# Half of the first layer's modulation products as dot products on VectorE, woven with the other half on TensorE

## The chip, the cores and the metric

The kernel runs on one core of one Trainium2 chip. The metric is the device time of one execution in microseconds (us): 2820.16 us as the median of 3 runs of the kernel before, which lie between 2816.92 and 2826.93 us. Everything is computed in 32-bit floats, or in pairs of high and low parts that stand for them.

## The reference, cut to what matters

The network has two layers of a first kind (mixers of attention, retention and gated linear attention) and then two layers of a second kind (attention and a feed-forward part, with a context stream beside the main one). Each layer of the first kind scales and shifts its input, and gates its output, by three vectors that depend on a condition c alone:

```python
c_act = jax.nn.silu(c)                      # 1 x 1024
# in layer l:
mod = c_act @ w_mod[l] + b_mod[l]           # 1024 by 3072 matrix
shift, scale, gate = jnp.split(mod, 3)
h = rms_norm(x, pre_gain) * (1.0 + scale) + shift
... y = mixers(h @ w_in) @ w_out
x = x + gate * rms_norm(y, post_gain)
```

The second kind does the same with six vectors a layer out of `ada_w`, for a condition and for a context condition. So a layer of the first kind needs a vector times a 12 MB matrix, and the vector is the same all through. None of it depends on x, so it can be computed long before its layer begins.

## The kernel before, in words

Activations stand with the 1024 features in 8 groups of 128 partitions and the 512 tokens along the row. Each weight block of 128 outputs is loaded as 512 KB on SP's queue (`weights`, L413 to 425), split by ScalarE into a high part (`wh`) and by GpSimd or VectorE into a low part (`wl`), and multiplied three times for each group of features (`dense`, L389 is the line of every matmul).

The first layer's `start` computes its own shift and scale. All later modulation vectors are made in the background: `mods` (L732) is a generator, and each call of `tick` from the loop that weaves the foreground work (`weave`) adds a rate to a counter and takes as many steps of the generator as the counter holds. A step is one load of the matrix on SP's queue (L750) into a tile `mr` of 128 partitions by 4 by 256 floats, 512 KB, from a ring of three. Two of them hold 256 columns of the matrix for all 1024 rows. `mod_sum` (L708) multiplies them on TensorE: the condition vector, in 32 columns of which one or two are used, is the weight, the matrix streams past, and four strips of 32 partitions of one PSUM tile hold partial sums. The second piece is multiplied first. `mod_take` (L719) copies the sums to SBUF on ScalarE (`ms`), `mod_cols` (L724) adds the strips and turns them into columns with small matmuls by `mod_sel`, and VectorE adds the bias (L741). Both PSUM tiles are of the tag `b`, which has two buffers for the whole kernel; the pairwise products of the gated linear attention use the same two.

During the first layer, `run` gives the background 24 such blocks: 4 for the gate of layer 0 (group 2 of `w_mod[0]`), 12 for all of layer 1 (groups 1, 0, 2 of `w_mod[1]`) and 8 for the first two groups of `ada_w[0]`, one after the other, at 0.76 steps per tick. In the foreground stand the gated linear attention (`gla`), woven with the projections and the retention (`layer1`), and after it the windowed attention, woven with half of the output projection. The gated linear attention goes through pairs of tiles: GpSimd multiplies (L1116, `pg`), ScalarE and VectorE split into `qb` (L1100, L400), TensorE multiplies into a `b` tile, VectorE copies it under a mask into the accumulator (L1135, `oy`). The results of the background are needed when the boundary to layer 1 (gate of layer 0, shift and scale of layer 1) and the norm of the context stream begin; the ring belongs to a memory area (`mp`) that is closed before that.

The order in each engine's queue is not the order of the program text alone: a planner goes through the instructions by priority (the order of the text, with shifts by hand), with costs of its own for each, and gives out the buffers of a ring as they come free in its own account of time. The engines then run their queues in that fixed order.

Of the kernel before, what the change touches and what calls it, by code (L numbers as in the profile page):

```python
# [11 lines left out]
F32 = mybir.dt.float32  # L12
# [4 lines left out]
AF = mybir.ActivationFunctionType  # L17
ALU = mybir.AluOpType
# [4 lines left out]
D = 1024  # L23
KD = D // 128
# [24 lines left out]
def _block1_cols():  # L49
    r = np.arange  # L50
    o = O1
    fm = [o["gq"] + r(128), o["gk"] + r(128)]
    fm += [heads(o["rq"], range(4), X1A), heads(o["rq"], range(4), X2A)]
    fm += [heads(o["rk"], range(4), X1A), heads(o["rk"], range(4), X2A)]
    fm += [np.r_[heads(o["ak"], range(2), X1A), heads(o["ak"], range(2), X2A)]]
    for g in range(2):
        fm += [heads(o["aq"], range(4 * g, 4 * g + 4), X1A), heads(o["aq"], range(4 * g, 4 * g + 4), X2A)]
    fm += [o["gg"] + i * 128 + r(128) for i in range(2)]
    fm += [o["rg"] + i * 128 + r(128) for i in range(2)]
    fm += [o["ag"] + i * 128 + r(128) for i in range(4)]  # L60
    tm = [np.r_[o["gv"] + r(256), o["ga"] + r(16)], np.r_[o["rv"] + r(256), o["av"] + r(128)]]
    return fm, tm
# [31 lines left out]
def _modw(w, n=256):  # L94

    return w.reshape(KD, 128, -1, n).transpose(2, 1, 0, 3)


def _modw_start(w):
# [9 lines left out]
def _xt(x):  # L109
    return x.reshape(x.shape[-2], KD, 128).transpose(2, 1, 0)  # L110
# [89 lines left out]
class Net:  # L200
# [531 lines left out]
    def mods(self, m, wsrc, groups):  # L732
        nc = self.nc
        outs, b, vecs = m

        def finish(t, g, q):
            o = self.mod_cols(t)
            w = slice(g * KD + 2 * q, g * KD + 2 * q + 2)
            for i, (_, n) in enumerate(vecs):
                if g < n:  # L740
                    nc.vector.tensor_add(outs[i][:, w], o[:, :, i], b[:, w])  # L741

        last = None
        for g in groups:
            for q in range(4):
                pieces = []
                for p in range(2):
                    raw = self.tl(self.mp, [128, 4, 256], F32, "mr", 3)
                    yield
                    nc.sync.dma_start(raw, wsrc[4 * g + q, :, 4 * p:4 * p + 4, :])  # L750
                    pieces.append(raw)
                t = self.mod_take(self.mod_sum(pieces, vecs, (1, 0)), self.mp, 2)
                if last is not None:
                    finish(*last)
                last = t, g, q
        yield
        finish(*last)

    def gain1(self, gain, scale, name):

        t = self.common.tile([128, KD], F32, tag=name, name=name)
        self.nc.vector.scalar_tensor_tensor(t, scale, 1.0, gain, op0=ALU.add, op1=ALU.mult)
        return t
# [1006 lines left out]
    def run(self):  # L1770
        nc, I = self.nc, self.I
# [4 lines left out]
        m1 = self.mod1  # L1776
        ada = [self.mods_new(I["ada_b"][l], 6, [("c_2", 6), ("c_ctx_2", (6, 2)[l])], f"ada{l}") for l in range(2)]
        m, mc = (self.mods2(0, ada[0][0][i], "xy"[i]) for i in range(2))
        with self.phase("c1") as self.c1:
            self.cp = self.vp = self.c1  # L1780
            mp = self.phase("mp")
            self.mp = mp.__enter__()
            self.background(self.chain(self.mods(m1[0], I["w_mod"][0], (2,)), self.mods(m1[1], I["w_mod"][1], (1, 0, 2)),
                                       self.mods(ada[0], I["ada_w"][0], (1, 0))), 0.76)
            mix = self.run_through(self.layer1(0, h, ready))
            self.stage(low=3)
            self.setup2()
            self.drain()
            mp.__exit__(None, None, None)
            with self.phase("ctx") as ph:  # L1790
                done = {}
                with self.phase("xc") as px:
                    xc = px.tile([128, KD, CL], F32, name="xc0")
                    nc.sync.dma_start(xc, I["ctx"])
                    y, sq = self.weave((self.out_proj(I["w_out"][0], mix[0], S, *mix[1:]), 8, 0),
                                       (self.keep(done, self.prenorm_steps(xc, CL, *mc(0), pool=ph)), 9, 0))
                scc, win, lat = self.even_project(done["result"], CL, 0, False, ph)
                h = self.weave((self.boundary(y, sq, I["x"], self.post_mod1(0), self.pre_mod1(1), x1), 18, 0), (win(), 4.5, -200))
                self.close_y()
                layer = self.layer1(1, h, {})  # L1800
                self.weave((self.first(layer, 3), 3, -200), (lat(), 11.0, 0))
            self.stage(low=3, mods=300)
            with self.phase("mp") as self.mp:
                self.background(self.mods(ada[0], I["ada_w"][0], (2,)), 0.5)
                mix = self.run_through(layer)
                self.drain()
        self.stage(low=3)
        with self.phase("c2") as self.c2:
# [3 lines left out]
            mp = self.phase("mp")  # L1812
# [16 lines left out]
            with self.phase("evp") as ph:  # L1829
                sc, win, lat = self.even_project(h, S, CL, True, ph)  # L1830
                self.weave((win(), 4.8, 0), (self.postnorm_steps(xc, yc, sqc, CL, mc(1)), 12.0, 0))
                o = self.oy(S)
# [25 lines left out]
            m, mc = (self.mods2(1, ada[1][0][i], "xy"[i]) for i in range(2))  # L1858
            with self.phase("ctx") as cx:
                with self.phase("ffn") as ph:  # L1860
# [3 lines left out]
                    f = self.ffn(0, h, S, hid)  # L1864
# [4 lines left out]
                _, val, diff, keys, _ = self.odd_project(done["result"], CL, 0, False, cx)  # L1869
# [3 lines left out]
        with self.phase("odd") as ph:  # L1873
            o = self.oy(S)
# [42 lines left out]
def _layout(a):  # L1917
    f1, (ta, tb) = _block1_cols()
    sq = np.arange(D).reshape(KD, 128)
    fo, to = _odd_cols()  # L1920
    uq = [np.concatenate([96 * h + np.arange(64) for h in (2 * i, 2 * i + 1)]) for i in range(4)]
    uq += [np.concatenate([96 * h + 64 + p for h in range(8)]) for p in (P1, P2)]
    ukv = np.concatenate([128 * h + np.arange(64) for h in range(8)] + [128 * h + 64 + np.arange(64) for h in range(8)])
    qn = a["od_qk_norm_2"][0]
    r = {
        "x": _xt(a["x"]), "c": a["c"].reshape(KD, 128).T, "positions": a["positions"].reshape(1, S),
        "w_mod_start": _modw_start(a["w_mod"][0]),
        "w_mod": np.stack([_modw(w) for w in a["w_mod"]]),
        "b_mod": _vec(a["b_mod"], 3 * KD).transpose(1, 0, 2),
        "pre_gain": _vec(a["pre_norm_gain"]), "post_gain": _vec(a["post_norm_gain"]),  # L1930
        "w_in": np.stack([_fm(w, f1) for w in a["w_in"]]),
        "w_tok_a": np.stack([_units(w, ta) for w in a["w_in"]]),
        "w_tok_b": np.stack([_units(w, tb) for w in a["w_in"]]),
        "attn_sinks": a["attn_sinks"].reshape(1, 16),
        "gla_gate_w": a["gla_gate_w"], "gla_gate_b": a["gla_gate_b"],
        "gla_gain": np.tile(a["gla_norm_gain"], (1, 2)).T,
        "w_out": np.stack([_fm(w, sq) for w in a["w_out"]]),
        "c_2": a["c_2"].reshape(KD, 128).T, "c_ctx_2": a["c_ctx_2"].reshape(KD, 128).T,
        "ctx": _xt(a["ctx_2"]),
        "ada_w": np.stack([_modw(w) for w in a["ada_w_2"]]),  # L1940
        "ada_b": _vec(a["ada_b_2"], 6 * KD).transpose(1, 0, 2),
        "norm_g": a["norm_g_2"].reshape(2, 4, KD, 128).transpose(3, 0, 1, 2),
        "ffn_w_in": np.stack([_fm(w, np.arange(2 * FH).reshape(-1, 128)) for w in a["ffn_w_in_2"]]),
        "ffn_w_out": np.stack([_fm(w, sq) for w in a["ffn_w_out_2"]]),
        "ev_w_in": _fm(a["ev_w_in_2"][0], _even_cols()),
        "ev_sink": a["ev_sink_2"].reshape(1, 8),
        "mla_gain": np.concatenate([a["ev_q_norm_2"][0].reshape(2, 128), a["ev_kv_norm_2"]]).T,
        "ev_w_uq": _fm(a["ev_w_uq_2"][0], uq).transpose(1, 0, 2, 3),
        "ev_w_ukv": a["ev_w_ukv_2"][0][:, ukv],
        "ev_w_out": _fm(a["ev_w_out_2"][0], sq),  # L1950
        "od_w_in": _fm(a["od_w_in_2"][0], fo),
        "od_w_tok0": _units(a["od_w_in_2"][0], to[0]), "od_w_tok1": _units(a["od_w_in_2"][0], to[1]),
        "qk_gain": np.stack([np.tile(qn[0][X1B], 4), np.tile(qn[0][X2B], 4), np.tile(qn[1][X1B], 4),
                             np.tile(qn[1][X2B], 4), np.r_[np.tile(qn[1][X1B], 2), np.tile(qn[1][X2B], 2)]], 1),
        "od_lambda": a["od_lambda_2"].reshape(1, 256),
        "subln": a["od_subln_2"].T,
        "od_w_out": _fm(a["od_w_out_2"][0], sq),
    }
    r.update(_consts())
    return {k: np.ascontiguousarray(v) for k, v in r.items()}  # L1960
# [22 lines left out]
```

## Time and profile before

| what | value |
|---|---|
| median of 3 runs | 2820.16 us |
| the profiled execution | 2819.89 us |
| its span, first to last instruction | 2818.1 us |
| mean granted TensorE clock | 0.918 of full speed |
| loads of `w_mod` in the background | 32 of 512 KB, issued from 101.2 to 311.3 us |
| loads of `ada_w` in the background of the first layer | 16 of 512 KB, issued from 311.7 to 411.4 us |

Engines are called PE (TensorE), PEld (its weight loads), DVE (VectorE), ACT (ScalarE), POOL (GpSimd) and SP (the queue that issues the DMAs) in the profile. A group of instructions is named by the line of the kernel, the engine, the operation and what is written from what (`b<-mr,mc` is a PSUM tile `b` from a matrix piece and the condition vector). L389, L398 and L400 are lines of helpers that many places use; the names of the tiles tell these apart. A wait is put down to the engine whose signal came last.

### The profile page before, as it was taken

The page shows a single profiled execution, that of the slowest core. Times are in us where ns is not written, and L with a number is a line of the kernel's source. Part 1 is how long each engine was busy: PE and PEld are TensorE (multiplying, and loading weights), DVE is VectorE, ACT ScalarE, POOL GpSimd, SP SyncE. Part 2 cuts the span into 40 slices and gives each one's busy share as a digit, 9 for nine tenths or more (in the row PEclk, how much of TensorE's full clock was granted, in tenths as well). Part 3 has the DMA queues.
Part 4 walks back from the last instruction along what each step waited for, and adds up shares of the span by engine and source line. Part 5 has one row for each costly group of instructions (what it writes and reads, how often), then busy time and mean ns, then how long its engine had stood idle before and what let it go on. Part 6 is the DMA issues. An engine that isn't in the chain of part 4 may idle for free. (4 is left out here: it accounts for less than half of the span.)

```text
span 2818.1 us, 35394 instructions
## 1 busy us (share of the span) xinstructions
PE 2455.0 (87%) x13052; PEld 1994.9 (71%) x13052; DVE 1258.7 (45%) x2065; ACT 1188.2 (42%) x2227; POOL 1079.4 (38%) x754
## 2 busy tenths in 40 slices
PE   6988896778888886769999899999888989799997
PEld 4765666666666665648998777777776777688886
DVE  3655357235646644445442631212645767421212
ACT  3534365333547534445554522222434646332222
POOL 2435235344533551213455732322542222443334
PEclk9988998888979987879999999999988989899998
DMA  7364644344344652335553545454444253333332
GB/s 244 121 205 156 207 165 154 107 140 162 104 124 139 213 182 100 116 112 143 174 159 135 186 135 172 149 169 133 148 140 158 90 153 113 113 100 97 94 97 75
DMA packets 170816, 400.56 MB, mean 142 GB/s; under 512 B 19378, under 2 KB 60820, under 8 KB 167316
## 3 DMA queue, kind: packets, MB, share of 16 engines
q1 hardware_dynamic: 170644, 398.31, 43.7%
q8 instruction: 103, 1.69, 0.2%
q14 instruction: 69, 0.57, 0.1%
HBM read 339.85 MB, written 58.39 MB: 141 GB/s over the span
## 5 line engine op out<-in xcount | busy, mean ns | idle before, releaser
L398 POOL TENSOR_TENSOR wl<-wr,wh 128x1024 fp32r<-128x1024 f32 (+3 forms) x245 | 538.2, 2198 | 899.5 <-ACT wh L422 451.5
L422 ACT CAST wh<-wr 128x1024 fp32r<-128x1024 f32 (+3 forms) x367 | 353.8, 964 | 706.5 <-PE d L389 279.5
L389 PE MATMUL d<-hh,wh 128*128 128x512 f32 x960 | 398.4, 415 | 19.7 <-ACT hh L556 7.8
L389 PE MATMUL d<-hl,wh 128*128 128x512 f32 x960 | 394.0, 410 | 1.9 <-DVE hl L557 0.9
L389 PE MATMUL d<-hh,wl 128*128 128x512 f32 x960 | 263.5, 403 | 0.0
L400 DVE SCALAR_TENSOR_TENSOR wl<-wr,wh 128x1024 fp32r<-128x1024 f32 (+3 forms) x122 | 152.1, 1246 | 227.8 <-PE d L389 91.9
L389 PEld LDWEIGHTS d<-hh,wh 128*128 128x128 f32 x960 | 190.6, 199 | 62.2 <-ACT hh L556 8.4
L389 PEld LDWEIGHTS d<-hl,wh 128*128 128x128 f32 x960 | 189.7, 198 | 42.5 <-issue 2.5
L389 PEld LDWEIGHTS d<-hh,wl 128*128 128x128 f32 x960 | 185.0, 195 | 39.6 <-issue 1.6
L400 DVE SCALAR_TENSOR_TENSOR pg<-b,pg 128x512 fp32r<-128x512 f32 (+1 forms) x208 | 137.2, 665 | 68.7 <-ACT pg L404 67.2
L389 PE MATMUL b<-hh,wh 128*128 128x512 f32 x416 | 164.2, 395 | 0.0
L389 PE MATMUL b<-hl,wh 128*128 128x512 f32 x416 | 163.2, 392 | 0.0
L934 POOL TENSOR_TENSOR oy<-pg,pg 64x256 f32<-64x256 f32 (+1 forms) x72 | 57.7, 802 | 262.3 <-DVE pg L932 91.3
L404 ACT CAST pg<-b 128x512 fp32r<-128x512 f32 (+1 forms) x208 | 117.1, 570 | 80.2 <-PE b L909 68.2
L882 DVE TENSOR_REDUCE sm<-s 128x1 f32<-128x768 f32 (+3 forms) x144 | 120.7, 846 | 26.6 <-PE s L389 25.9
L389 PE MATMUL d<-hc,wh 128*128 128x256 f32 x656 | 105.4, 311 | 23.7 <-DVE rp L400 11.8
L950 DVE SCALAR_TENSOR_TENSOR rp<-rp,d 128x512 f32<-128x512 f32 (+1 forms) x77 | 46.7, 607 | 165.5 <-ACT rp L949 165.4
L1745 DVE SCALAR_TENSOR_TENSOR rp<-rp,b 128x512 f32<-128x512 f32 (+1 forms) x64 | 38.1, 595 | 175.3 <-PE b L389 174.8
L389 PE MATMUL d<-hid,wh 128*128 128x512 f32 (+1 forms) x528 | 114.7, 361 | 1.5 <-POOL hid L398 1.5
L389 PEld LDWEIGHTS d<-hc,wh 128*128 128x128 f32 x656 | 94.9, 211 | 28.3 <-ACT wh L422 12.2
L389 PE MATMUL b<-hid,wh 128*128 128x512 f32 (+1 forms) x528 | 110.8, 361 | 0.0
L389 PE MATMUL b<-hh,wl 128*128 128x512 f32 x416 | 103.8, 389 | 0.0
(416 smaller groups left out, 5143.2 us busy)
## 6 DMA issues: line engine op xcount, KB each, us to landing
wr<-in_ffn_w_in SPq DMA_DIRECT2D x132, 512.0 KB
mr<-in_ada_w SPq DMA_DIRECT2D x96, 512.0 KB
wr<-in_ffn_w_out SPq DMA_DIRECT2D x48, 512.0 KB
x<-x SPq DMA_DIRECT2D x20, 1024.0 KB
wr<-in_w_in SPq DMA_DIRECT2D x38, 512.0 KB
mr<-in_w_mod SPq DMA_DIRECT2D x32, 512.0 KB
wr<-in_ev_w_in SPq DMA_DIRECT2D x20, 512.0 KB
wr<-in_ffn_w_out SPq DMA_DIRECT2D x24, 384.0 KB
```

What stands on the lines that cost most here:

```text
L389: self.nc.tensor.matmul(out, lhsT, rhs, start=start, stop=stop)
L398: self.nc.gpsimd.tensor_sub(out, src, hi)
L400: self.nc.vector.scalar_tensor_tensor(out, src, scale, hi, op0=ALU.mult, op1=ALU.subtract)
L404: self.nc.scalar.copy(hi, src)
L422: nc.scalar.copy(hi[:, :n], raw[:, :n])
L882: nc.vector.reduce_max(c, s, axis=AX.X, negate=True)
L934: nc.gpsimd.tensor_tensor(d, sel(t), sel(rs), op=ALU.mult)
L950: nc.vector.scalar_tensor_tensor(t, t, 1.0, ps, op0=ALU.add, op1=ALU.mult)
L1745: nc.vector.scalar_tensor_tensor(g, g, 0.5, pu, op0=ALU.mult, op1=ALU.mult)
```

## The change

In the first layer's background the 12 blocks of layer 1 leave `mods`. A new generator, `mods_rows`, computes them as dot products. The matrix is laid out in memory by output (`w_mod_rows`: 24 slabs of 128 outputs by 1024 inputs), so an output is a partition and its inputs lie along the row. The condition vector is loaded once into all 128 partitions; ScalarE's Tanh and a VectorE operation make its activation. Each half slab (128 by 512 floats, 256 KB) is loaded into `mr`, and one VectorE operation multiplies it by the vector and writes the sum over the row into a column of the result, or of `part` for the second half; two small additions per group of eight columns add the bias and the second half. That is 48 loads and 48 such operations.

The other 12 blocks stay with `mods`, but in the first layer with pieces of two row groups (256 KB) instead of four, `self.mk = 2`, so a block takes four loads. Both generators are woven one step each, share one ring of four 256 KB buffers, and run at 1.55 steps per tick. After the first layer `mk` is 4, with 512 KB pieces in a ring of three as before; there, too, the pieces are now multiplied in the order in which they are loaded.

```diff
-                for p in range(2):
-                    raw = self.tl(self.mp, [128, 4, 256], F32, "mr", 3)
+                n = self.mk
+                for p in range(KD // n):
+                    raw = self.tl(self.mp, [128, n, 256], F32, "mr", (4, 3)[n // 4])
                     yield
-                    nc.sync.dma_start(raw, wsrc[4 * g + q, :, 4 * p:4 * p + 4, :])
+                    nc.sync.dma_start(raw, wsrc[4 * g + q, :, n * p:n * p + n, :])
                     pieces.append(raw)
-                t = self.mod_take(self.mod_sum(pieces, vecs, (1, 0)), self.mp, 2)
+                t = self.mod_take(self.mod_sum(pieces, vecs, range(KD // n)), self.mp, n // 2)
...
+    def mods_rows(self, m, wsrc, groups, src):
+
+        nc = self.nc
+        (out,), b, _ = m
+        row, t = self.tl(self.mp, [128, D], F32, "row", 1), self.tl(self.sb, [128, D], F32, "wr", 3)
+        nc.sync.dma_start(row, src.to_broadcast([128, D]))
+        nc.scalar.activation(t, row, AF.Tanh, scale=0.5)
+        nc.vector.scalar_tensor_tensor(row, t, 1.0, row, op0=ALU.add, op1=ALU.mult)
+        for g in groups:
+            w = slice(g * KD, g * KD + KD)
+            part = self.sm([128, KD])
+            for f in range(KD):
+                for p in range(2):
+                    raw = self.tl(self.mp, [128, D // 2], F32, "mr", 4)
+                    yield
+                    d = slice(D // 2 * p, D // 2 * (p + 1))
+                    nc.sync.dma_start(raw, wsrc[g * KD + f, :, d])
+                    o = part[:, f:f + 1] if p else out[:, g * KD + f:g * KD + f + 1]
+                    nc.vector.scalar_tensor_tensor(raw, raw, 0.5, row[:, d], op0=ALU.mult, op1=ALU.mult, accum_out=o)
+            nc.vector.tensor_add(out[:, w], out[:, w], b[:, w])
+            nc.vector.tensor_add(out[:, w], out[:, w], part)
...
-            self.mp = mp.__enter__()
-            self.background(self.chain(self.mods(m1[0], I["w_mod"][0], (2,)), self.mods(m1[1], I["w_mod"][1], (1, 0, 2)),
-                                       self.mods(ada[0], I["ada_w"][0], (1, 0))), 0.76)
+            self.mp, self.mk = mp.__enter__(), 2
+            by_rows = self.mods_rows(m1[1], I["w_mod_rows"], (1, 0, 2), I["c_row"])
+            by_cols = self.chain(self.mods(m1[0], I["w_mod"], (2,)), self.mods(ada[0], I["ada_w"][0], (1, 0)))
+            self.background(self.woven((by_rows, 48, 0), (by_cols, 51, 0)), 1.55)
...
             mp.__exit__(None, None, None)
+            self.mk = 4
```

## Rows read from the trace of the kernel before

**Rows 1.** The page, part 1: busy us, share, instructions.

```profile
PE 2455.0 (87%) x13052; PEld 1994.9 (71%) x13052; DVE 1258.7 (45%) x2065; ACT 1188.2 (42%) x2227; POOL 1079.4 (38%) x754
```

**Rows 2.** The chain of waits that ended last, by line, shares of the span.

```profile
by line: PE b L389 0.6%; PE d L389 0.5%; DVE bp L576 0.2%; DVE x L577 0.1%; PE s L498 0.0%; PE s L389 0.0%; POOL sm L483 0.0%; DVE oy L625 0.0%; ACT rp L503 0.0%; issue 0.0%; DVE sm L481 0.0%
```

**Rows 3.** Stretches 95:312 and 312:455, summed: busy us of each engine.

```profile
sum 360.00, PE 312.30 PEld 234.54 DVE 192.02 ACT 166.45 POOL 155.06; mean PE 156.15 PEld 117.27 DVE 96.01 ACT 83.22 POOL 77.53
```

**Rows 4.** The same view in 5 us steps, with PEclk, DMA share, GB/s.

```profile
140.00:145.00 5.00, 5.00 (x29) 4.75 (x28) 3.72 (x5) 3.53 (x8) 2.45 (x3) 1.00 0.79 264
160.00:165.00 5.00, 0.79 (x1) 0.29 (x1) 0.74 (x3) 2.01 (x5) 1.74 (x1) 0.55 0.91 329
440.00:445.00 5.00, 5.00 (x24) 4.14 (x23) 4.42 (x8) 2.92 (x6) 4.08 (x4) 1.00 0.30 105
```

**Rows 5.** TensorE's waits, 95 to 455 us: total us, times, longest.

```profile
PE b L389 <- DMA mr<-in_w_mod: 7.3, 3, 3.7
PE b L389 <- DVE oy L1135: 6.9, 5, 2.2
PE d L389 <- ACT wh L422: 5.9, 1, 5.9
PE b L498 <- DVE rp L495: 4.0, 2, 2.3
PE b L389 <- DVE rp L518: 3.3, 1, 3.3
PE b L389 <- DVE pg L1190: 3.2, 1, 3.2
...
PE d L389 <- DVE pg L400: 2.0, 3, 1.3
...
PE d L389 <- DVE rp L950: 1.7, 1, 1.7
```

**Rows 6.** TensorE's groups, 95 to 455 us: busy, mean ns | idle.

```profile
L389 PE MATMUL b<-mr,mc 128*32 128x256 f32 x384 | 35.7, 430 | 12.8 <-DMA mr<-in_w_mod 7.3 <-DVE pg L1190 3.2 <-DVE oy L1135 2.1
L389 PE MATMUL b<-mod_sel,ms 128*128 128x2 f32 x96 | 16.4, 276 | 0.3 <-DVE oy L1135 0.2
```

**Rows 7.** ScalarE's groups, the same view and stretch.

```profile
L721 ACT COPY ms<-b 128x256 f32<-128x256 f32 x24 | 8.9, 370 | 18.9 <-PE b L389 18.4
...
L887 ACT ACTIVATION_READ_ACCUMULATOR wp<-s,sm 128x1 f32 x32 | 6.6, 207 | 0.0
```

**Rows 8.** VectorE's groups, the same view and stretch.

```profile
L400 DVE SCALAR_TENSOR_TENSOR rp<-rp,rp 128x512 f32<-128x512 f32 x9 | 9.6, 1061 | 9.1 <-ACT rp L404 5.7 <-ACT rp L406 2.7
...
L400 DVE SCALAR_TENSOR_TENSOR pg<-b,pg 128x512 fp32r<-128x512 f32 x14 | 9.4, 681 | 2.5 <-ACT pg L404 2.5
...
L1313 DVE SCALAR_TENSOR_TENSOR oy<-oy,rp 128x512 f32<-128x512 f32 x8 | 5.4, 690 | 4.2 <-POOL oy L934 2.4 <-DMA rp<-gate 1.8
...
L400 DVE SCALAR_TENSOR_TENSOR wl<-wr,wh 128x512 fp32r<-128x512 f32 x5 | 3.7, 737 | 4.8 <-PE d L389 4.6 <-ACT wh L422 0.3
...
L400 DVE SCALAR_TENSOR_TENSOR hl<-oy,hh 128x512 fp32r<-128x512 f32 x4 | 2.8, 695 | 1.1 <-ACT hh L404 1.1
...
L741 DVE TENSOR_TENSOR m<-b,m1b 128x2 f32<-128x2 f32 x12 | 1.9, 158 | 26.1 <-PE b L389 26.1
...
L400 DVE SCALAR_TENSOR_TENSOR la<-pg,la 128x512 fp32r<-128x512 f32 x1 | 1.1, 1125 | 0.0
```

**Rows 9.** VectorE's groups, the same view from 0 to 100 us.

```profile
L400 DVE SCALAR_TENSOR_TENSOR u12l<-wr,u12h 128x1024 fp32r<-128x1024 f32 x1 | 1.2, 1226 | 0.8 <-ACT u12h L422 0.8
```

**Rows 10.** Line 750, 95 to 455 us: ns min/median/max, first and last start.

```profile
L750 SPq DMA_DIRECT2D mr<-in_w_mod x32: 327/383/3162, 101.2 to 311.3; - x32
L750 SPq DMA_DIRECT2D mr<-in_ada_w x16: 327/371/562, 311.7 to 411.4; - x16
```

**Rows 11.** SP's queue, its own waits from 95 to 455 us.

```profile
SPq L417 <- POOL wl L398: 61.6, 15, 8.9
SPq L750 <- PE b L389: 61.5, 24, 9.4
```

More of the change, by code (lines that the diff above doesn't have):

```diff
@@ L96, in _modw, with _modw_rows @@
     return w.reshape(KD, 128, -1, n).transpose(2, 1, 0, 3)
+def _modw_rows(w):
+    return w.T.reshape(-1, 128, D)
 def _modw_start(w):
@@ L1927, in _layout @@
         "w_mod_start": _modw_start(a["w_mod"][0]),
-        "w_mod": np.stack([_modw(w) for w in a["w_mod"]]),
+        "w_mod": _modw(a["w_mod"][0]), "w_mod_rows": _modw_rows(a["w_mod"][1]), "c_row": a["c"].reshape(1, D),
         "b_mod": _vec(a["b_mod"], 3 * KD).transpose(1, 0, 2),
```

## Prediction

> **What bounds the kernel now.** I read the page first. TensorE is busy for 87% of the span, VectorE 45%, ScalarE 42%, GpSimd 38% [rows 1]: TensorE is the engine that most work queues for. The chain of waits was next, and the reader is to see that it doesn't help here: it reaches back over the last feed-forward only and holds about 1% of the span [rows 2]. What an edit in the first layer is worth must be read from that stretch itself. The loads that the change touches are issued from 101 us on, and the last products on them run near 420 us, so I took 95 to 455 us as the stretch. In its 360 us TensorE is busy for 312.3, VectorE 192.0, ScalarE 166.5, GpSimd 155.1 [rows 3]; 47.7 us of TensorE are idle. That is a mean over two sorts of time. In steps of 5 us from 140 to 460 us, 23 of the 64 show TensorE busy for 4.9 us or more (140:145 is the first of them, 440:445 the last); the others have a hole, the worst at 160 us with 0.79 us of work, after which the granted clock stands at 0.55 [rows 4]. So TensorE time that is freed moves the end forward at once in 36% of this stretch; elsewhere it first of all widens a hole. The waits of TensorE say who makes the holes: VectorE for 6.9, 4.0, 3.3, 3.2, 2.0 and 1.7 us (21.1 together), the modulation loads for 7.3 us in 3 waits, a late weight cast for 5.9 us once [rows 5].
>
> **The change part by part.** Of the 24 products of a 1024 by 256 block with the condition vector that this stretch holds (4 for the first layer's gate, 12 for the second layer's three groups, 8 for ada), the 12 of the second layer leave TensorE and come back as 48 dot products on VectorE.
>
> *What goes.* 12 of 24 products: half of 35.7 us for the wide matmuls and half of 16.4 us for the small ones that turn the sums into columns [rows 6], 17.9 + 8.2 = 26.0 us of TensorE. Half of ScalarE's 24 evictions of the sums: 4.4 us of work and 9.2 us of waiting for TensorE [rows 7]. On VectorE the 12 bias additions: 1.9 us of work, but 26.1 us in which the engine stood before them waiting for TensorE [rows 8]. Of TensorE's 7.3 us on late loads, 12 of the 16 products on w_mod are these: 5.5 us.
>
> *What comes.* Each dot is a scalar_tensor_tensor of 128x512 floats, both tensors in SBUF, with a sum written out as well. Rows of this size and kind in the stretch run from 0.69 us (oy from oy and rp, x8) to 1.06 us (rp from rp and rp, x9); all five groups together are 22.6 us in 27, 0.84 us each [rows 8]. With one input in PSUM the same operation takes 0.68 us [rows 8]. The trace has no such sum on VectorE. Its cost lies between 0 and the 0.207 us of ScalarE's own read of an accumulator [rows 7]; I take 0.15 us, near the 0.158 us of VectorE's smallest operations here [rows 8]. So 48 x 0.99 = 47.5 us; the ends are 48 x 0.69 = 33.1 and 48 x (1.06 + 0.21) = 60.9 us. Preparing the vector once is one 128x1024 operation, 1.2 us by [rows 9], six small additions are 0.9 us, which makes 49.6 us for VectorE; ScalarE has one pass over that vector more, which the sum leaves out.
>
> The gap between 0.68 and 1.06 us is where GpSimd comes in, whose subtractions work beside these rows. The Trainium skill (SBUF — State Buffer, "Who interferes with whom") says that a VectorE instruction with two SBUF inputs and a GpSimd instruction that reads SBUF shut each other out, the later one waiting for the whole of the earlier. The trace agrees as far as a mean of 1.06 us against 0.68 us can show it [rows 8]. By the rule every one of the 48 dots can also hold up a GpSimd subtraction for its 0.7 us, which the sum below doesn't charge. The skill also says (VectorE: DVE Perf Modes, "Two Vector instructions with no wait between them") that an operation which writes out its accumulator is two instructions; no row of before shows that on VectorE.
>
> *What waits.* A dot now stands at the head of VectorE's queue until its load has landed. Behind it wait the splits of the gated linear attention (qb), which TensorE needs, and the masked copies, which free its two PSUM banks. I let the 5.5 us of load waits that TensorE loses come back in full on VectorE. The ends are 0 (a dot is needed by nobody before 450 us and may be placed late) and the 26.1 us that the additions waited. Net, VectorE's queue carries 49.6 + 5.5 - 1.9 - 26.1 = 27.1 us more.
>
> *The loads.* The bytes are the same, but there are 96 loads of 256 KB for 48 of 512 KB. An issue takes 0.37 to 0.38 us [rows 10], so SP works 18 us more in 360. Of those 96, the column products still need four pieces at once, in a ring of four that the dots share, 1 MB in place of 1.5 MB. SP stands on that ring already: 61.5 us in 24 waits for TensorE to give a buffer back; what queues behind it are the weight loads and the copies of q, k and v, and 61.6 us more are waits of the weight loads for GpSimd [rows 11]. The smaller ring is worth between minus 5 us (a buffer comes free after one dot, not after 16 matmuls) and one more late weight, 5.9 us, for every weight load that slips; I take nothing, since each end has about as much behind it. The later stages keep 512 KB pieces in a ring of three, multiplied in the order of arrival and no longer the second one first; no wait of TensorE for an ada load is among its long ones [rows 5], so I take nothing.
>
> *The sum, against the profiled execution (2819.89 us; span 2818.1 and 1.8 around it).* TensorE: 26.0 x 0.36 = 9.4 us forward (ends 0 and 26.0). Its waits for loads: of 5.5 us I keep half, since in the holes another releaser is close behind: 2.8 us (ends 0 and 5.5). Banks: 24 fewer tenants of the two PSUM banks for which TensorE waited 6.9 us behind the masked copies [rows 5]; a fifth of it, 1.4 us (ends 0 and 6.9). ScalarE: its releases cost TensorE 5.9 us in the largest wait for 166.5 us of work, 0.036 per us; 13.6 us less give 0.5 us. VectorE: 21.1 us of TensorE's holes are its doing for 192.0 us of work, 0.11 per us; 27.1 us more cost 3.0 us (ends: below nothing, if the 26.1 us of standing is worth more than the dots, and 33 us, if half of 60.9 + 5.5 + 2.1 - 1.9 us falls into holes and nothing of the standing comes back). 9.4 + 2.8 + 1.4 + 0.5 - 3.0 = 11.1 us less: 2808.8 us. The median of the runs, 2820.16 us, is 0.3 us above that execution, so the same number stands for both.
>
> **The rivals.**
> *TensorE is the bound throughout (chance 0.15).* All 26.0 us and the 5.5 us come off, VectorE costs its 3.0: 2791 us. For it: 87% busy [rows 3]. Against: 41 of 64 steps have a hole.
> *The freed time stays idle (0.18).* The holes belong to the chain through VectorE, ScalarE and GpSimd; less filler on TensorE only widens them, and after a hole the clock is low [rows 4], which slows the rest. Gains of 2.8 us against the cost of 3.0: 2820 us.
> *VectorE takes over (0.10, slower).* The place is the gated linear attention, 100 to 310 us: a dot of 1.06 + 0.21 us, often behind a GpSimd instruction, ahead of qb splits and masked copies. Price 33 us less the 9.4 and 2.8 gained: 2841 us. It decides once TensorE's waits for VectorE grow from 21.1 us past about 35 us. Against: VectorE would be at (192 + 50 - 2) / 360 = 67%, below TensorE.
> *The ring of four holds SP (0.07, slower).* Three late weights at 5.9 us more than eat the gain: 2819.9 - 11.1 + 17.7 = 2826.5, to 2832 us with a fourth.
> What has its chance left is the forecast, 0.50, with its own range of 2800 to 2817 us. The instructions are set into their queues by a planner with a model of time, so other holes of 3 to 6 us come and go; that is this range's width.
>
> **How the numbers follow.** A difference under 0.3% (8.5 us) is no more than a measurement of this kernel can tell from no change. Faster than that is below 2811.7 us: 0.6 of the forecast's 0.50 and the first rival, 0.45. Slower, above 2828.6: VectorE, most of the ring, and a little of the idle case, 0.19. Between lies 0.36. The range 2790 to 2830 us holds the first and second rival, the forecast and half of the ring's case; outside are VectorE's case and the tails.
>
> **What would show it.** Right: TensorE's products on modulation loads in this stretch fall from 35.7 to about 18 us and the small ones from 16.4 to about 8; 48 dots near 1.0 us; the 26.1 us of VectorE before the second layer's additions gone, with a few us of waits for loads in its place; the out-projection of the first layer starting about 10 us earlier. Wrong in size: the same busy times, but TensorE's idle up by what its work fell. Wrong in sign: waits of TensorE for VectorE past 35 us, dots over 1.2 us, or SP's waits on the ring well past 61.5 us with ScalarE's casts late behind them.

## The result and the profile after

The changed kernel takes 2839.47 us (median of 4 runs, 2838.05 to 2842.06). Beside it the kernel before took 2820.4 us. The ratio is 1.0065, 95% interval 1.0039 to 1.0092: slower by some 18 us, where 11 us less were forecast, and outside the range. The profiled execution has a span of 2840.3 us, 22 us above the one of before, at a granted clock of 0.914 of full speed against 0.918.

All of it is lost by the end of the first layer. The products of the windowed attention begin at 360.7 us, where they began at 342.9 us; the norm of the context stream starts at 449.7 us instead of 431.7 us, and the second half of the layer's normed output (`bp` from `y`, L581, L576 before) at 481.2 us instead of 459.5 us. The transposes at 2165 us and the end are later by the same 21 to 22 us. Part 1 of the page of the changed kernel, which answers to [rows 1] (busy us, share of the span, instructions):

```profile
PE 2446.1 (86%) x12812; PEld 1992.9 (70%) x12812; DVE 1300.0 (46%) x2156; ACT 1186.2 (42%) x2216; POOL 1085.4 (38%) x754
```

The stretch that answers to [rows 3] is 20 us longer, 95 to 475 us. Its line of sums, from 95:330 and 330:475:

```profile
sum 380.00, PE 302.96 PEld 228.80 DVE 232.05 ACT 165.26 POOL 159.58; mean PE 151.48 PEld 114.40 DVE 116.02 ACT 82.63 POOL 79.79
```

TensorE has 9.3 us less to do than in [rows 3] and stands idle for 77.0 us instead of 47.7. Its work on the modulation, in the groups of the stretch that answer to [rows 6] (busy us, mean ns | idle before):

```profile
L394 PE MATMUL b<-mr,mc 128*32 128x256 f32 x192 | 22.2, 402 | 6.5 <-DMA mr<-in_w_mod 3.1 <-DVE oy L1163 1.9 <-DMA mr<-in_ada_w 1.3
...
L394 PE MATMUL b<-mod_sel,ms 128*128 128x2 f32 x48 | 6.8, 245 | 0.8 <-ACT pg L959 0.8
```

The halves are gone, 23.1 us where 26.0 were forecast. But TensorE's work fell by 9.3 us only: the rest of it takes some 14 us more than before, at a lower mean granted clock. The same view over the whole stretch (the column behind POOL is the clock), the kernel before and the changed one:

```profile
95.00:455.00 360.00, 312.30 (x1708) 234.54 (x1707) 192.02 (x346) 166.45 (x378) 155.06 (x143) 0.91 0.53 173
95.00:475.00 380.00, 302.96 (x1473) 228.80 (x1471) 232.05 (x440) 165.26 (x370) 159.58 (x143) 0.88 0.52 170
```

The dots themselves, by their line (ns min/median/max, first and last start), with what the engine waited for ahead of them:

```profile
L783 DVE SCALAR_TENSOR_TENSOR mr<-mr,row x48: 651/692/2637, 112.8 to 430.7; 128x512 f32<-128x512 f32 x48
L783 DVE DVE_READ_ACCUMULATOR mr<-mr,row x48: 71/81/85, 114.2 to 431.3; 128x1 f32 x48
...
its engine sat idle before it (us, times) until:
  DMA mr<-in_w_mod_rows: 22.4, 11
```

So a dot is two instructions, 0.69 and 0.08 us in the median; with the slow ones, up to 2.64 us, it is 0.88 + 0.08 = 0.96 us in the mean. The reader is to see the last line: VectorE stood for 22.4 us in 11 waits for loads. TensorE's waits, which answer to [rows 5] (total us, times, longest), have changed hands with that:

```profile
PE b L394 <- DVE pg L1218: 8.4, 4, 6.7
PE b L394 <- ACT ms L726: 7.2, 2, 6.8
PE d L394 <- DVE rp L978: 7.2, 1, 7.2
PE d L394 <- ACT wh L427: 6.2, 1, 6.2
PE b L394 <- DVE oy L1163: 5.5, 3, 3.2
PE d L394 <- POOL pg L403: 4.9, 6, 1.8
```

All of the waits for VectorE together are 35.3 us, by the same sum 21.7 us before. How one of them comes about is seen in the order of time. VectorE's instructions there (start us, duration, instruction, and in brackets the wait before it):

```profile
243.43 0.74 DVE L1163 COPY_PREDICATED oy<-gla_mask,b 128x512 f32<-128x512 uint8 x1
251.04 0.69 DVE L783 SCALAR_TENSOR_TENSOR mr<-mr,row 128x512 f32<-128x512 f32 x1 [6.87 <-DMA mr<-in_w_mod_rows]
...
251.82 0.28 DVE L1218 TENSOR_TENSOR pg<-b,rq 128x128 f32<-128x128 f32 x1
```

And TensorE's in the same view:

```profile
245.09 0.40 PE L394 MATMUL d<-hh,wl 128*128 128x512 f32 x1
252.16 1.01 PE L394 MATMUL b<-gla_w,la 128*128 128x384 f32 x2 [6.67 <-DVE pg L1218]
```

A dot that nobody needs before 450 us stands at the head of VectorE's queue for 6.87 us. Behind it is a product of 0.28 us that frees a PSUM bank, and TensorE stands for 6.67 us. The ring on SP's queue answers to [rows 11]:

```profile
SPq L422 <- POOL wl L403: 51.2, 14, 8.4
SPq L781 <- DVE mr L783: 26.6, 11, 4.8
SPq L756 <- DVE mr L783: 22.4, 10, 6.0
SPq L781 <- PE b L394: 21.5, 12, 4.4
SPq L756 <- PE b L394: 20.5, 8, 10.1
```

The modulation loads now stand for 91.0 us until VectorE or TensorE gives a buffer back, in 41 waits, against 61.5 us in 24 for TensorE alone before. Counted with their waits for anything else, an earlier load into the same buffer above all, it is 111.4 us against 93.7 us.

### The profile page after: what moved, and what is told of

Read it like the earlier page. It is cut to its first block, busy times and chain, and to the rows that moved or that the text cites. A ratio compares the mean times of both kernels' runs of the same rounds, so it can differ in the third digit from the quotient of the medians.

```text
span 2840.3 us, 35090 instructions
## 1 busy us (share of the span) xinstructions
PE 2446.1 (86%) x12812; PEld 1992.9 (70%) x12812; DVE 1300.0 (46%) x2156; ACT 1186.2 (42%) x2216; POOL 1085.4 (38%) x754
```

## The experiments

Ratios are to the kernel before, run on the same chip beside each. The second row takes over at once the changed kernel's pieces, ring, weaving and rate, its order of the pieces, and one buffer for `ms` in place of two (`n // 2` in the change); each row behind it adds one thing. The planner lays out the queues of every kernel anew, and a step holds what comes of that too:

| kernel | ratio, 95% interval | step, of 2820 us |
|---|---|---|
| the 12 blocks' products out, loads as before | 0.9940 (0.9919 to 0.9961) | -16.9 |
| their loads as 48 of 256 KB, all pieces of 256 KB in a ring of four, no dots | 0.9989 (0.9974 to 1.0005) | +13.8 |
| and the dots, not waiting for loads | 1.0005 (0.9992 to 1.0018) | +4.5 |
| and the preparation of the vector | 1.0015 (0.9996 to 1.0033) | +2.8 |
| and the waits: the changed kernel | 1.0065 (1.0039 to 1.0092) | +14.1 |

A step is the difference of two such ratios and uncertain by some 6 to 7 us (9 us for the last). The second and the last are more than that, the third and fourth are not.

**What the freed TensorE time is worth: `loads_big`, `left_out`.** In the kernel before, the layer's blocks keep their loads and lose products, evictions and additions.

```diff
                     pieces.append(raw)
+                if skip:
+                    continue
```

> The kernel before, with the products of layer 1's 12 blocks left out (their result is the bias) and all 48 loads kept as they were: 512 KB each, in the ring of three, one after the other. With layer 1's blocks left out altogether the time was 2809 us; with their loads alone, in the changed kernel's 256 KB pieces and ring of four, 2822 us. Theory R, the smaller pieces in the smaller ring, shared by two streams, cost the 12 us: here 2809 to 2812 us. Rival L, any 12 MB of loads here cost what freed TensorE time gives, or freed time beside loads gives nothing: 2818 to 2822 us.

2805.04 us, 0.9940. With the old ring and 512 KB pieces the relief is worth 17 us. TensorE's busy time in 95 to 455 us is 300.1 us, 12 us below [rows 3]. In `left_out` the changed kernel has neither dots nor their loads:

```diff
+            nc.vector.tensor_copy(m1[1][0][0], m1[1][1])
+            by_rows = iter([None] * 48)
```

> As the changed kernel, but the 12 blocks of layer 1 are left out altogether: no preparation, loads or dots (their result is the bias). What is left is the gain of 12 products fewer on TensorE and 12 MB less to load, the best that any placing of the dots could reach. The forecast's terms give 13.6 us less than before: 2807 us. If freed TensorE time stays idle: 2817 to 2821 us. If TensorE were the bound throughout: 2789 us.

2808.99 us, 0.9949 (0.9927 to 0.9971). So with the work left out altogether some 14 to 17 us come off, and the change had to stay below that with all it adds.

**The loads alone: `loads_only`.** The changed kernel without dots and without the vector; the 48 loads go into the ring and nothing reads them.

```diff
-                    nc.vector.scalar_tensor_tensor(raw, raw, 0.5, row[:, d], ...)
```

> As the changed kernel, but without preparation and without dots: the 48 loads stay, woven into the ring of four (layer 1's modulation is left out). If the loads cost nothing beside others, as forecast: 2809 us, as with layer 1's blocks left out. If the smaller ring and SP's queue cost: 2814 us or more. The difference to the kernel with neither preparation nor waits is the busy time of the dots, forecast as 50 us less 28 of standing at 0.11, some 3 us; by a VectorE bound 8 to 15 us.

2821.88 us, 0.9989. Of the 17 us, 14 are gone without one dot. Beside `left_out`, which already has the small pieces, the ring of four and the rate for the 12 blocks that stay, these 48 loads alone cost 11.3 us (0.9989 against 0.9949, uncertain by some 8 us).

**The dots without waits: `no_wait`, `neither`.** The dots multiply halves of the resident vector with each other, so that no load is waited for; the loads stay.

```diff
-  ...scalar_tensor_tensor(raw, raw, 0.5, row[:, d], ..., accum_out=o)
+  ...scalar_tensor_tensor(self.pg([128, D // 2]), row[:, D // 2 * (1 - p):D // 2 * (2 - p)], 0.5, row[:, d], ..., accum_out=o)
```

> As the changed kernel, but each dot multiplies the resident row by itself, with its product in a work tile: the 48 loads stay, and no dot waits for one (the modulation of layer 1 is left out in value). VectorE's time in dots stays near 46 us. Theory A, VectorE standing before dots for late loads (22.4 us in 11 waits) is what holds TensorE at 245 to 300 us: about 10 to 12 us less, 2828 us. Theory B, the dots' busy time and their meetings with GpSimd: no more than 3 us less, 2836 to 2840 us.

2827.74 us, 1.0015. The waits are worth 14 us, 0.6 us of end for each of the 22.4 us that VectorE stood. SP's standing doesn't explain the step: its 49.0 us of waits until a dot gives a buffer back become 49.6 us of waits until the load before it in the same buffer has landed. `neither` has the vector from GpSimd as well, with no load and no Tanh:

```diff
-        nc.sync.dma_start(row, src.to_broadcast([128, D]))
-        nc.scalar.activation(t, row, AF.Tanh, scale=0.5)
-        nc.vector.scalar_tensor_tensor(row, t, 1.0, row, op0=ALU.add, op1=ALU.mult)
+        nc.gpsimd.memset(row, 0.5)
```

> As the changed kernel, with neither the preparation of the vector (a constant row) nor a wait of a dot on its load (each dot multiplies the row by itself); the 48 loads and the 48 dots' time stay (layer 1's modulation is left out in value). In the kernel without preparation alone, VectorE stood 9.5 us before the first dot where ScalarE and VectorE had stood for the preparation, so each hides the other's delay of 8 us. Theory A2: with both gone the q copies of the retention go out near 121 us as before and the whole takes 8 us less than without waits alone, 2820 us. Rival: the 8 us stem from the loads' place in SP's queue; then 2826 to 2829 us.

2824.29 us, 1.0005, where 2820 us were expected. Its dots take VectorE 42.3 us; beside `loads_only` they cost about 4.5 us, 0.11 us for each, with an uncertainty larger than the cost.

**The preparation alone: `no_prelude`.** The last edit by itself, with the dots' waits kept.

> As the changed kernel, but the row that the dots read is set to a constant by GpSimd: the load of c into 128 partitions, its Tanh on ScalarE and its scaling on VectorE are left out, and with them the weight buffer that the Tanh writes into (the modulation of layer 1 is then not c's). Theory A, the preparation of the vector stops the first weight load and ScalarE at 92 to 104 us and costs about 8 us for good: 2831 us, and TensorE's hole of 6.2 us at 104 to 110 us gone. Theory B, the dots' own time on VectorE is the loss, and what is late at 110 us is made good later: 2837 to 2840 us.

2840.89 us, 1.0062 (1.0043 to 1.0081): nothing is gained. In the changed kernel, by ScalarE's instructions in order of time, the engine stands for the vector, and the weight whose buffer the Tanh took comes late:

```profile
103.41 1.06 ACT L771 ACTIVATE wr<-row 128x1024 f32<-128x1024 f32 x1 [5.59 <-DMA row<-in_c_row]
108.97 1.04 ACT L427 CAST wh<-wr 128x1024 fp32r<-128x1024 f32 x1 [4.51 <-DMA wr<-in_w_in]
```

In `no_prelude`, by VectorE's instructions in the same view, VectorE stands at that place for the first dot's load, and TensorE for 7.6 us behind it:

```profile
107.18 0.69 DVE L781 SCALAR_TENSOR_TENSOR mr<-mr,row 128x512 f32<-128x512 f32 x1 [9.47 <-DMA mr<-in_w_mod_rows]
```

Each hides the other; of these kernels with dots only `neither`, without both, has its first copy of q at 121.6 us as before (122.2), against 130.6 us in the changed kernel. Of these 9 us the step at the end shows 2.8 us, less than its uncertainty, where 8 were expected.

**Can the waits be moved? `low_dots60`, `one_after_other`.** The dots 60 places later in the planner's priority, or the two generators one after the other.

```diff
-                    nc.vector.scalar_tensor_tensor(raw, raw, 0.5, row[:, d], ...)
+                    with self.ahead(-60):
+                        nc.vector.scalar_tensor_tensor(raw, raw, 0.5, row[:, d], ...)
```

```diff
-            self.background(self.woven((by_rows, 48, 0), (by_cols, 51, 0)), 1.55)
+            self.background(self.chain(by_rows, by_cols), 1.55)
```

> The whole changed kernel, each dot with a priority 60 places lower, so that the planner sets other ready VectorE work before it. Theory A: if this puts the dots later against their loads, VectorE's 22.4 us of standing shrink by half and the time falls by some 5 us, to 2834 us. If the planner sets a dot as soon as VectorE is free by its own account of when the load lands, nothing changes: 2839 us.

> The whole changed kernel, but the two generators run one after the other, first the 48 dots, then the 12 blocks of products, in the same ring of four at the same 1.55 steps per tick. While the dots run, no block holds up to four buffers for its sum, so their loads can run up to four ahead: if it is the sharing that makes the dots' loads late, VectorE's 22.4 us of standing fall to under 10 and the time to 2828 to 2832 us. If the loads are late because of the queue of transfers alone, or the blocks with four buffers to themselves lose what the dots gain: 2837 us or more.

The first takes 2834.21 us, 1.0038 (1.0020 to 1.0056), with 15.7 us of waits in 9; the second 2843.41 us, 1.0071 (1.0044 to 1.0097), with 28.3 us in 8. The weaving isn't what costs, and a later place helps in part at most. In `low_dots60` all of TensorE's waits for VectorE are 21.6 us, as many as before, and 11 us of loss stay: those waits are not the whole of it.

**The ring alone: `small_ring`, `ring_six`.** The kernel before, all products on TensorE, with the changed ring in the first layer; then with six buffers, the 1.5 MB of before.

```diff
-                for p in range(2):
-                    raw = self.tl(self.mp, [128, 4, 256], F32, "mr", 3)
+                for p in range(KD // n):
+                    raw = self.tl(self.mp, [128, n, 256], F32, "mr", (4, 3)[n // 4])
...
-                t = self.mod_take(self.mod_sum(pieces, vecs, (1, 0)), self.mp, 2)
+                t = self.mod_take(self.mod_sum(pieces, vecs, range(KD // n)), self.mp, 2)
```

The second pair of lines is the order of the loads, as in the changed kernel.

> The whole kernel before, computed as before, but in the first layer its 24 blocks come in pieces of 256 KB from a ring of four buffers (1 MB for 1.5 MB), at 1.5 steps per tick for 0.76. Theory R: the pieces and the ring cost 8 to 12 us by themselves, 2828 to 2833 us. Rival L: the loads cost by their bytes; 2818 to 2823 us.

> The kernel before with 256 KB pieces as in small_ring, but six buffers in place of four: 1.5 MB, as the three of 512 KB held. Theory R1, it is the bytes that the ring can hold ahead of the products: most of small_ring's 18 us come back, 2820 to 2825 us. Theory R2, it is twice as many loads in SP's queue, in pieces of half the size: 2833 us or more.

2840.74 us, 1.0081 (1.0053 to 1.0109), and 2835.21 us, 1.0047 (1.0031 to 1.0062). The ring that the prediction took at nothing loses by itself as much as the whole change. In the group of products on it, 95 to 475 us in `small_ring`, the count and mean are those of [rows 6]; the busy time isn't:

```profile
L389 PE MATMUL b<-mr,mc 128*32 128x256 f32 x384 | 48.3, 429 | 16.4 <-DMA mr<-in_w_mod 10.9 <-DVE oy L1136 3.3 <-DVE qb L400 1.5
```

The same 384 matmuls hold TensorE for 48.3 us instead of 35.7, and 40.6 us in `ring_six`: they overlap less. In order of time they stand in 36 unbroken stretches before, mostly the 16 records of a block, in some 56 in `small_ring` and 46 in `ring_six`, where a block is broken up more often. The smaller pieces don't do that by themselves: `left_out` has them and the ring of four for half the blocks, and its 192 matmuls take 17.6 us in 18 stretches, half of before. The Trainium skill (TensorEngine Tiling (Array Packing), "Key Properties") says that a change of the tiling mode drains TensorE; these matmuls (128*32) stand among others (128*128), so more stretches would be more changes. That fits these three; no run here separates it from other reasons, and `ring_two` below has 39.3 us in 37 stretches.

**Which part of small pieces: `split_issue`, `paired_six`, `ring_two`.** First before's ring and steps, each 512 KB buffer filled by two transfers; then six small buffers, taken two to a step at before's 0.76 steps; then two buffers of 512 KB.

```diff
-                    nc.sync.dma_start(raw, wsrc[4 * g + q, :, 4 * p:4 * p + 4, :])
+                    for s in range(self.mk):
+                        e = slice(4 // self.mk * s, 4 // self.mk * (s + 1))
+                        nc.sync.dma_start(raw[:, e, :], wsrc[4 * g + q, :, 4 * p + e.start:4 * p + e.stop, :])
```

> The kernel before with its ring of three buffers of 512 KB and its steps, but in the first layer each buffer is filled by two transfers of 256 KB. If the number of transfers in SP's queue makes the loss of small pieces, this is slower like the ring of six (1.0047 in ratio, about 2834 us against 2821). If the steps and the ring's hand-over make it, this is within 0.2% of before (2816 to 2827 us).

> The ring of six buffers of 256 KB, with two pieces taken in one step at 0.76 steps per tick, so that the background moves in before's steps. If the finer steps (where the planner puts them among the foreground) make the loss, this is back at before (2816 to 2827 us); if the number of transfers or the hand-over buffer by buffer, it stays at the ring of six (2830 to 2840 us).

> The kernel before with a ring of two buffers of 512 KB in the first layer instead of three: the bytes of the changed kernel's ring, with before's pieces. If the ring's bytes were the loss, it is slower by some 0.8% like four buffers of 256 KB (about 2843 us); if small pieces were, it loses only the difference between the rings of four and six, about 5 us (2822 to 2830 us).

2837.56 us, 1.0061 (1.0044 to 1.0079); 2839.66 us, 1.0067 (1.0050 to 1.0085); 2859.19 us, 1.0139 (1.0119 to 1.0160). Splitting the transfers, with ring, buffers and steps as before, is enough to lose 17 us, and the finer steps show no part in it. The split also halves the packets of these loads, by the trace's counts for this stretch 33300 packets in all for 60.9 MB instead of 26550 for 62.0 MB, so whether the number of transfers or the size of their packets costs is not separated. I had expected the ring's bytes to cost 5 us; with two buffers of 512 KB in place of three they cost 39. SP's queue shows where the split hurts early on. The kernel before, in order of time (start, time from the first issue of a row to the end of its last, how many):

```profile
141.13 3.43 SPq L816 DMA_DIRECT2D rk<-rp  x4
144.67 3.16 SPq L750 DMA_DIRECT2D mr<-in_w_mod  x1
153.39 3.57 SPq L819 DMA_DIRECT2D rk<-rk  x4
157.01 1.05 SPq L1029 DMA_DIRECT2D tab<-angles  x2
158.11 7.87 SPq L417 DMA_DIRECT2D wr<-in_w_in  x4
166.07 0.38 SPq L816 DMA_DIRECT2D rv<-rp  x1
```

And `split_issue` at the same place:

```profile
141.67 3.43 SPq L818 DMA_DIRECT2D rk<-rp  x4
145.19 3.52 SPq L752 DMA_DIRECT2D mr<-in_w_mod  x2
154.61 4.80 SPq L821 DMA_DIRECT2D rk<-rk  x4
159.47 1.05 SPq L1031 DMA_DIRECT2D tab<-angles  x2
160.62 10.20 SPq L417 DMA_DIRECT2D wr<-in_w_in  x4
170.91 0.38 SPq L818 DMA_DIRECT2D rv<-rp  x1
```

The same issues stand in the same order, two transfers in the place of one, and the rows behind are longer: 4.80 for 3.57 us, 10.20 for 7.87 us, so that the copy of v starts 4.8 us later. The issues in these rows are not longer: by their lines each copy of k takes 0.44 to 0.59 us and each weight 0.33 to 0.43 us in both kernels. SP stands longer between them until earlier transfers have landed. Its waits for transfers (total us, times, longest) from the modulation load to the copy of v, in the kernel before (144.7 to 166.1 us):

```profile
SPq L819 <- DMA rk<-rp: 6.7, 2, 5.5
...
SPq L417 <- DMA wr<-in_w_in: 2.6, 1, 2.6
```

And in `split_issue` (145.2 to 170.95 us):

```profile
SPq L821 <- DMA rk<-rp: 8.3, 2, 5.8
SPq L417 <- DMA wr<-in_w_in: 4.9, 1, 4.9
```

Later places can't be read like this, because the order of the queues differs as well (TensorE's from about 120 us on): the planner counts transfers too. How much of the 17 us are late transfers and how much that order stays open.

**The answer put to the changed kernel: `after_big`.** 512 KB pieces in both halves, two buffers, 24 dots of 128 by 1024.

```diff
-                for p in range(2):
-                    raw = self.tl(self.mp, [128, D // 2], F32, "mr", 4)
...
+                raw = self.tl(self.mp, [128, D], F32, "mr", 2)
...
-            self.background(self.woven((by_rows, 48, 0), (by_cols, 51, 0)), 1.55)
+            self.background(self.woven((by_rows, 24, 0), (by_cols, 26, 0)), 0.78)
```

> The changed kernel with pieces of 512 KB in both halves, ring of two buffers (the same 1 MB), 24 dot products of 128 by 1024 instead of 48 of 128 by 512. If the small pieces are the failed step, it gains most of their 14 us against the changed kernel: 2822 to 2830 us. If the bytes of the ring or the waits of the dot products for loads decide, it stays at 2835 us or above; a piece twice as large lands later, so that the waits can also grow.

2842.32 us, 1.0079 (1.0062 to 1.0096): my expectation failed. By `ring_two` two buffers are too few. But beside `ring_two`, which has the same two buffers and no dots, it is 17 us faster; beside `small_ring` the changed kernel is 4.5 us faster, less than its uncertainty. On an equal ring of two the move to VectorE is worth something; the smaller ring costs more. The dots with before's ring of three were not run in this layer.

**The order of the pieces: `order`.** The kernel before with the first piece multiplied first everywhere.

```diff
-                t = self.mod_take(self.mod_sum(pieces, vecs, (1, 0)), self.mp, 2)
+                t = self.mod_take(self.mod_sum(pieces, vecs, (0, 1)), self.mp, 2)
```

> The kernel before, with one edit: the two 512 KB pieces of each block are multiplied in the order of their loads, (0, 1), everywhere. As forecast, nothing: 2820 us within 4. If the second piece is now waited for in mid-product while a PSUM bank is held: 5 to 10 us more, spread over all background stages.

2830.09 us in the median, but a ratio of 1.0011 (0.9990 to 1.0032). It is inconclusive: at most 9 us. The changed kernel, which has the new order everywhere, loses nothing behind the first layer by its trace. The trace of `order`, its slowest execution, is 8.4 us late at `bp` (467.9 us for 459.5) and 16 us at the end, so a cost in either place isn't excluded.

**The same move where TensorE has no holes: `ffn_dots`.** In the feed-forward stage, the kernel before computes 24 blocks of the second `ada_w`, with TensorE busy for 412.5 of 420 us (1560 to 1980 us). Four of its six groups become 32 dots of 128 by 1024, ring of three, 512 KB pieces; the first layer is as before.

```diff
-                    self.background(self.mods(ada[1], I["ada_w"][1], (1, 0, 2, 4, 3, 5)), 1.3)
+                    by_rows = self.mods_rows(ada[1], I["ada_rows"], (2, 4, 3, 5), I["c_row"])
+                    by_cols = self.mods(ada[1], I["ada_w"][1], (1, 0))
+                    self.background(self.woven((by_rows, 32, 0), (by_cols, 17, 0)), 1.3)
```

> The kernel before, with the same idea in another place: in the feed-forward part of the first layer of the second kind, groups 2 to 5 of ada_w[1] (16 blocks for one condition) become 32 dots of 128x1024 on VectorE, woven with the 8 blocks that stay, in the ring of three 512 KB buffers. There TensorE is busy for 412.5 of 420 us (1560 to 1980 us in the trace of before) and VectorE for 118. A block costs TensorE (25.7 + 14.5) / 24 = 1.67 us. Theory A (a dot costs when VectorE's queue leads to TensorE, TensorE's freed time counts where it has no holes): 16 x 1.67 = 26.8 us less, 2793 us, 2800 with some new holes. Rival (dots on VectorE delay the splits here too): no gain, 2815 us or more.

2798.89 us, 0.9911 (0.9887 to 0.9935): faster than both kernels. VectorE stands longer for loads than in the changed kernel. Its largest wait in that stretch (total us, times, longest):

```profile
DVE mr L775 <- DMA mr<-in_ada_rows: 59.4, 23, 4.7
```

And TensorE's two largest there:

```profile
PE b L389 <- POOL wl L398: 4.6, 2, 2.3
PE b L389 <- DVE rp L518: 2.7, 1, 2.7
```

The 59.4 us of standing hardly reach TensorE: all its waits for VectorE in that stretch are 3.1 us, against 0.4 us before, and of the 26.8 us that the 16 blocks' products take 25 came off, with an uncertainty of some 7 us.

## Why the prediction was wrong

- **TensorE's freed time: right in sum.** 14.1 us forecast, 16.9 us measured by `loads_big`; no run measured its terms one by one. The largest has a slip: 23 full steps of 64 count from 140 us on, but the nine from 95 to 140 us are full as well, 32 of 72 in the stretch; with that share the term is 11.6 us in place of 9.4. In the changed kernel the products fell by 13.4 us instead of 17.9, as their blocks are broken up more often and overlap less (27 unbroken stretches for 192 matmuls, by the measure of before 18); the small ones by 9.7 instead of 8.2. And the rest of TensorE's work took some 14 us more, at a granted clock of 0.88 for 0.91, which no term of the sum has; a low clock after holes stands only with a rival.
- **The duration of a dot: right.** 0.99 us forecast, 0.96 us measured. (The upper end of 1.06 us passes over the one row of 1.13 us in [rows 8]; nothing hung on it.) The accumulator's read is 0.08 us, where 0.15 was taken; the Trainium skill (VectorE: DVE Perf Modes, "Two Vector instructions with no wait between them") counts it as an instruction of its own, and the rows show it as one. The price of VectorE's work, 0.11 us of end for each us, has nothing against it: 0.11 from `neither` beside `loads_only`, but within an interval that holds 0 too.
- **The loads at nothing: the step that failed.** The prediction saw 96 loads for 48 and a ring of 1 MB for 1.5 MB, and set a buffer's earlier release against a late weight. `loads_only` puts 14 us on that step (11 us on the 48 loads alone), `small_ring` 23 us for all blocks, `split_issue` 17 us for the doubled transfers in the kernel before. The step priced what a transfer costs SP to issue, 0.37 us, and that is about right: 0.43 us in the median of `split_issue`. What it left out is what twice the transfers do to those behind them: where it could be followed, SP stood for 13.2 us instead of 9.3 us until earlier copies and weights had landed.
- **The waits of the dots: right in kind, wrong in size.** 5.5 us were taken, within ends of 0 and 26.1; it is 22.4 us. And they were priced like work, 0.11 us each, but cost 0.6, with an uncertainty of 0.4. The wait at 251 us shows how: the release of a PSUM bank stands behind the dot. That the planner counts on a dot's work but not on its load being late is the likely reason why such a place was chosen, and not shown.
- **The preparation of the vector** was left out but for VectorE's part. It delays a weight by its buffer, and in the changed kernel is hidden by the first dot's wait; 2.8 us, within the uncertainty, without those waits.
- **The rivals.** *VectorE takes over* gave 2841 us and its sign, waits of TensorE for VectorE past 35 us, came (35.3); but its price was the dots' work in the queue, and that is cheap, and its other sign, dots over 1.2 us, stayed away (0.96). *The ring of four holds SP* named the place, 7 in 100, and 2826.5 to 2832 us; by `small_ring` it is nearer the mechanism, and the waits for loads came on top of it. The late weights that it counted on aren't seen: TensorE waits once for a late cast, 6.2 us, as before (5.9). Neither alone is the cause. The sum of forecast terms with the two measured in place of the two failed ones is -14.1 + 13.8 + 3.0 + 14.1 = +16.8 us (18 measured).

What stays open: how the doubled transfers' 17 us divide between transfers that land late and the order that the planner makes of them, whether the number of transfers or their packets' size counts, and why the ring alone costs 23 us with products on both halves and 14 us with one.

## What to carry to other kernels

Before work moves to an engine that does it as fast, price the ring that feeds it: its pieces, its buffers and the number of transfers are worth as much here as the engine time that is moved, or more. A load's consumer is put on an in-order queue where nothing urgent stands behind it: 22.4 us of standing cost 14 us in the first layer, 59.4 us in the feed-forward stage left 25 us of a gain of 26.8, though other things differ there too. And the relief alone, with the work left out and all else kept, shows in one run what a move can win at most.

## What the runs showed of the hardware

- A VectorE operation with a summed output is followed by a read of its accumulator of 71 to 85 ns.
- With two inputs in SBUF the dot took 692 ns in the median and 2637 ns at most. This agrees with the Trainium skill (SBUF — State Buffer, "Who interferes with whom"), by which such an instruction and a GpSimd instruction that reads SBUF shut each other out; GpSimd's groups are beside it in the same stretch, but no run takes them away.
- The same 384 matmuls of 128*32 took 35.7 us of TensorE in 36 unbroken stretches, 40.6 us in 46 and 48.3 us in some 56 (`before`, `ring_six`, `small_ring`).
- With twice the transfers and packets at the same bytes the kernel took 17 us more, of 2820, the planner's new order included (`split_issue`). An issue stayed at 0.38 to 0.43 us in the median (maxima 3.16 and 2.90 us); the waits for landings behind them grew, 9.3 to 13.2 us at the place shown.
